# A ring of twenty weight buffers instead of eighteen, and a cap on the loads ahead of a loop

## The chip, the cores and the metric

The kernel runs on one core of a Trainium2 chip. Times are device microseconds (us) of one execution; the metric is the median of several runs.

## The reference

One layer of a streaming encoder, float32, on 256 frames and 16 meta tokens, width 1024. A mixer (differential attention beside a state-space model) and a layer norm come first. Then comes a mixture of 32 experts, of which each token takes four:

```python
gate = xb @ w_gate[e] + b_gate[e]
up = xb @ w_up[e] + b_up[e]
gate = jnp.minimum(gate, SWIGLU_LIMIT)
up = jnp.clip(up, -SWIGLU_LIMIT, SWIGLU_LIMIT)
y = ((up + 1.0) * gate * jax.nn.sigmoid(gate * SWIGLU_ALPHA)) @ w_down[e] + b_down[e]
```

Each expert has three matrices of 1024 x 1024, so 96 matrices of 4 MB are read: 384 MB, once each. A second layer norm ends it.

## The kernel before, in words

**The stream of weights.** Each expert matrix is loaded in four pieces of 1 MB (256 rows of 1024 floats). Experts are sorted by load and worked off as positions t = 0 to 31; a position has three steps w: gate (0), up (1), down (2). `stream` lists the 384 pieces in the order of use: both input steps of position t, then the down step of position t - 1. `place` gives a piece's number in it. `place[28, 2, 3]` is 355 and `place[29, 1, 3]` is 351.

**The ring.** Piece c goes into entry c % NR of `ring` (line 488), where an entry is a half of a buffer slot; NR is 18. The first buffers to be free stand first, since most of them hold the mixer's operands ahead of the stream. `load_to(n)` (line 529) has SP issue pieces until n are out, in order. `chunk` (line 500) issues one (line 522; the last piece in two halves, line 525). Each waits until TensorE has used what lay in the buffer, and SP's queue does everything in program order, so a wait holds all loads behind it.

**Where loads are issued.** In the mixer, `load_to` is called with 2, 4, 6, 10, 12, 16 and 18 (lines 702 to 1001), each time where slots have just come free. In the expert part, every step calls it with the number of its own last piece plus 1 + NR (lines 1298 and 1339): as many pieces are out as the ring holds.

**The order of the engines' work.** The loop at the end of `hybrid_layer` writes it out by hand: for each t, the gate and up steps (`unit_in`), then the tokens of the next group are gathered (`prepare`, line 1118 for the matmuls), then the down step of t - 1 (`out_pos`). A step is `linear`: a matmul that puts in the bias (line 1150), then eight blocks of matmuls on the weights (line 1156), two blocks a piece. `add_rows` (line 1211) and, for the last position, lines 1327 and 1361 add an expert's rows to the tokens.

**The overflow loop.** Experts can get more tokens than their place in the plan has room for. `overflow` (line 1236) reads the count of such leftovers into every engine (line 1237) and runs a hardware loop over them (line 1238). It stands in `out_pos(28)` (LOOP_AT is 28), in the iteration t = 29, behind the loads that the steps of t = 29 call for. With these inputs the count is zero. After it come the two rows of the second layer norm (bc2, by `load`, line 128) and the loads of the last positions.

**Other names.** `Gt` (line 884) holds the gates of the chosen experts; `gates` writes it, `onehots` and `sort_b` read it. `rep` is scratch of `route_c`. The kernel is built with the default scratch space for descriptors of dynamic DMAs (line 1463).

Of the kernel before, what the change touches and what calls it, by code (L numbers as in the profile page):

```python
# [25 lines left out]
NE = 32  # L26
# [21 lines left out]
LOOP_AT = 28  # L48
# [16 lines left out]
def hybrid_layer(ctx, tc, I, out):  # L65
    nc = tc.nc
# [10 lines left out]
    def nb(n=1):  # L77
        b = bank[0]
        if b + n > 8:
            b = 0  # L80
        bank[0] = (b + n) % 8
        return b
# [44 lines left out]
    def load(dst, name, off, dims):  # L127
        return SP.dma_start(dst, pap(I[name], off, dims))
# [192 lines left out]
    for k in range(7):  # L321
        n = min(2 ** k, 68 - 2 ** k)
# [161 lines left out]
    def rows_of(kb):  # L484
        a = 256 * (kb // 2) + kb % 2
        return slice(a, a + 255, 2)

    ring = [(6, 0), (6, 1), (3, 0), (3, 1), (4, 0), (4, 1), (2, 0), (8, 0), (2, 1), (8, 1), (1, 0), (1, 1),
            (5, 0), (0, 0), (5, 1), (0, 1), (7, 0), (7, 1)]
    NR = len(ring)  # L490
    RT, CH, eid, npools = {}, {}, {}, {}
# [6 lines left out]
    place = {x_: c for c, x_ in enumerate(stream)}  # L498

    def chunk(c):  # L500
        t, w, j = stream[c]
        i, half = ring[c % NR]
        if i not in RT:
            if i == 7:
                t_ = npools["b"].tile([128, 4, D], F32, name="wx", tag="slot7")
                RT[i] = [t_[:, 0:2], t_[:, 2:4]]
            elif i in HALVED:
                RT[i] = [slot(f"{i}{c}", [128, 2, D], "wx") for c in "ab"]
            else:
                t_ = slot(i, [128, 4, D], "wx")  # L510
                RT[i] = [t_[:, 0:2], t_[:, 2:4]]
        CH[c] = RT[i][half]
        src = I[("w_gate", "w_up", "w_down")[w]]
        if t < 2:
            srcv = pap(src, t * D * D + j * 256 * D, [[2 * D, 128], [1, 2 * D]])
        else:
            if t not in eid:
                eid[t] = SP.value_load(EI[0:1, t:t + 1], min_val=0, max_val=NE - 1)
            srcv = src[0][ds(eid[t], 1), j * 256:(j + 1) * 256, :].rearrange("o (p k) f -> p (o k f)", p=128)
        dstv = CH[c].rearrange("p k f -> p (k f)")  # L520
        if c < len(stream) - 1:
            SP.dma_start(dstv, srcv)
        else:
            for k in range(2):
                SP.dma_start(dstv[:, k * D:(k + 1) * D], srcv[:, k * D:(k + 1) * D])
# [3 lines left out]
    def load_to(n):  # L529
        while nload[0] < min(n, len(stream)):  # L530
            chunk(nload[0])
            nload[0] += 1


    def split_w(j, s_, l_, ks):
# [75 lines left out]
    def values(h):  # L611
        vT = lw([128, NP], "vT", bufs=2)
        S.activation(vT, proj("v", h, 0), AF.Copy)
        return vT

    def value_rows(h, vT):
        b = nb()
        for blk, n in ((0, 128), (1, 128), (2, 16)):
            T.transpose(PS[:n, b, blk * 128:blk * 128 + 128], vT[:, blk * 128:blk * 128 + n], ident)
        S.activation(vr[:, 0:2, h * 128:(h + 1) * 128], PS[:, b, 0:256].rearrange("p (a e) -> p a e", a=2), AF.Copy)  # L620
        S.activation(vr[:16, 2, h * 128:(h + 1) * 128], PS[:16, b, 256:384], AF.Copy)
# [65 lines left out]
    def lag_b():  # L687
        KS = lt_([128, 4, 128], "KS", tag="y0")
        S.activation(KS, PS[:, kb_].rearrange("p (f c) -> p f c", f=4), AF.Copy)
        V.tensor_add(KS[:, :, 0:32], KS[:, :, 0:32], Dm)  # L690
        for j in range(4):
            for t in range(4):
                dst = ML[32 * t:32 * t + 32, :, j, 32 * t:128]
                srcv = KS[32 * j:32 * j + 32, :, 0:128 - 32 * t]
                if t < 2:
                    V.tensor_copy(dst, srcv)
                else:
                    S.activation(dst, srcv, AF.Copy)

    vt0 = values(2)  # L700
    lag_b()
    load_to(2)
    vt1 = values(3)
    wo0 = slot(3, [128, 4, D], "wo0")
    W_OUT[0] = [wo0[:, k] for k in range(4)]
# [9 lines left out]
    split_w(1, 5, 0, ((2, False, G), (3, False, G)))  # L715
    value_rows(2, vt0)
    value_rows(3, vt1)
    load_to(4)


    cat = mt([128, 8, NT], "cat", FR, tag="hTcat")
# [52 lines left out]
    def out_a(fb):  # L774
        b = nb()
        for j in range(4):
            P = 4 * fb + j
            o = PS[:64, b, j * 128:(j + 1) * 128]
            T.matmul(o, u4[:, P, 4:68], ML[:, fb, j], start=True, stop=False)
            for ri in range(2):  # L780
                T.matmul(o, XS[fb][:, ri, j, 3:67], AB[:, ri, P].rearrange("p t g c -> p (t g c)"),
                         start=False, stop=(ri == 1))
        yt = lt_([64, 512], "yt", bufs=2)
        S.activation(yt.rearrange("p (t a c) -> p a t c", t=4, a=4),
                     PS[:64, b].rearrange("p (a t c) -> p a t c", a=4, t=4), AF.Copy, scale=0.5)
        YT[fb] = yt
# [15 lines left out]
    def out_c(f2):  # L802
        hy, ya = HY[f2]
        for f in range(2):
            V.scalar_tensor_tensor(gy[:, 2 * f2 + f].rearrange("p (c t) -> p t c", t=4), ya[:, f], 1.0, hy[:, f],
                                   op0=OP.add, op1=OP.mult)
# [9 lines left out]
    out_b(0)  # L816
    out_a(2)
    out_a(3)
    load_to(6)
    out_c(0)  # L820
    av_c(1)
    out_b(1)
# [6 lines left out]
    def mix(i, kbs, fs=(0, 1)):  # L829
        for f in fs:  # L830
            for kb in kbs:
                o, q, k, c_ = PS[:, mb + 2 * i + f, :], kb // 4, kb % 4, slice(i * 128, (i + 1) * 128)
                f_ = slice(f * 512, (f + 1) * 512)
                T.matmul(o, cat[:, kb, c_], W_HI[q][k][:, f_], start=(kb == 0), stop=False)
                T.matmul(o, cat[:, kb, c_], W_LO[q][k][:, f_], start=False, stop=False)
                T.matmul(o, cl[q][:, k, c_], W_HI[q][k][:, f_], start=False, stop=(kb == 7))
# [38 lines left out]
    def wt(shape, name, dt=F32, tag=None, bufs=None):  # L875
        return wp.tile(shape, dt, name=name, tag=tag or name, bufs=bufs)
# [4 lines left out]
    jp, io = wt([128, 128], "jp", I32, tag="tabi"), wt([128, 128], "io")  # L881
    tri, one = wt([128, 128], "tri", BF), wt([128, 128], "one", BF)
    P96, s32 = wt([96, NE], "P96", BF), wt([128, 32], "s32")
    lg, M_, Gt, PM, ev, rep = (wt([128, 2, NE], n) for n in ("lg", "M", "Gt", "PM", "ev", "rep"))
    Mb = wt([128, 2, NE], "Mb", BF)
    m8, sm1, nm1 = wt([128, 2, 8], "m8"), wt([128, 2], "sm1"), wt([128, 2], "nm1")
    YC2 = wt([128, 2, D], "yc")
# [4 lines left out]
    for t in range(2):  # L892
        SI[t] = wt([96, 128], "si", BF, bufs=3)
    bc1 = [wt([128, D], "bc1", tag="xg", bufs=2) for _ in range(2)]
    load_to(10)
    load(bc1[0], "ln1_g", 0, [[0, 128], [1, D]])
    load(bc1[1], "ln1_b", 0, [[0, 128], [1, D]])
    load_to(12)


    G.iota(jp, pattern=[[1, 128]], base=0, channel_multiplier=-1)
# [8 lines left out]
    def selector(t, eng):  # L910
        m = max(u[4] for u in UNITS if u[0] == t)
        if t not in SI:
            SI[t] = wt([96, 128], "si", BF, bufs=3)
        eng.tensor_copy(SI[t][:, :m], P96[:, t:t + 1].to_broadcast([96, m]))  # L914
# [22 lines left out]
    def affine1(i, h, eng):  # L937
        hf = hr[:, i, h * 512:(h + 1) * 512]
        eng.tensor_tensor(hf, hf, bc1[0][:, h * 512:(h + 1) * 512], op=OP.mult)
        eng.tensor_tensor(hf, hf, bc1[1][:, h * 512:(h + 1) * 512], op=OP.add)  # L940
# [32 lines left out]
    def places(i):  # L973
        b = nb()
        if i:
            T.matmul(PS[:, b, :NE], one, Mb[:, 0], start=True, stop=False)
        T.matmul(PS[:, b, :NE], tri, Mb[:, i], start=(i == 0), stop=True)
        V.scalar_tensor_tensor(PM[:, i], M_[:, i], -4096.0, PS[:, b, :NE], op0=OP.mult, op1=OP.add)
# [13 lines left out]
    mix(1, (6,), (1,))  # L992
    turn1(0)
    mix(1, (7,), (1,))
    load_to(16)
    mid.close()
    tail = ExitStack()
    npools["b"] = tail.enter_context(tc.tile_pool(name="moeb", bufs=1, side="right", reuse_waits="tile"))
    acc = npools["b"].tile([128, 2, D], F32, name="acc", tag="acc")
    h1T = acc[:, 0].rearrange("p (k c) -> p k c", k=8)  # L1000
    load_to(18)
    affine1(0, 0, G)
    route_a(0)
    norm1(1)
# [7 lines left out]
    places(0)  # L1012
    route_c(1)
    places(1)

    RV, CO, KR = rk[:, 0:NE], rk[:, NE:NE + 3], rk[:, NE + 3:2 * NE + 3]
    tabs = lw([128, 3, 64], "tabs", tag="vT", bufs=2)
# [313 lines left out]
    for t in range(NE):  # L1331
        if 2 <= t + 1 < NE:
            selector(t + 1, G)
        for w in range(2):
            for u in pos_units[t]:
                unit_in(u, w)
            if (t, w) in between:
                between[t, w]()
            load_to(place[t, w, 3] + 1 + NR)
        for g in range(1, NG):  # L1340
            if first_pos[g] == t + 1:
                prepare(g, G)
        if t:
            out_pos(t - 1)
        if t == LOOP_AT + 1:
            bc2 = per.tile([128, 2, D], F32, name="bc2", tag="hr")
            load(bc2[:, 0, :], "ln2_g", 0, [[0, 128], [1, D]])
            load(bc2[:, 1, :], "ln2_b", 0, [[0, 128], [1, D]])

            m = GROUPS[-1][-1][1]  # L1350
            GL = YC2[:, NG % 2].rearrange("p (f c) -> p f c", f=4)
            G.memset(GL, 0.0)  # L1352
            for f in range(128 // m):
                S.activation(GL[f * m:f * m + m, f], GT[NG][:m], AF.Copy)

    (u_,) = pos_units[NE - 1]
    t, g, o, _, m = UNITS[u_]
# [14 lines left out]
    n = r_.shape[2]  # L1372
# [99 lines left out]
```

## Time and profile before

| | |
|---|---|
| median of 3 runs | 1189.6 us (1189.0 to 1190.3) |
| the profiled execution | 1188.67 us |
| its span, first to last instruction | 1186.9 us |
| TensorE matmuls busy | 1038.4 us (87%) |
| VectorE busy | 360.6 us (30%) |
| SP's DMA queue | 88.5% of 16 engines' span |
| read from HBM | 423.50 MB |
| mean granted TensorE clock | 0.952 |

PE is TensorE's matmuls, PEld its weight loads, DVE VectorE, ACT ScalarE, POOL GpSimd, SP the engine that issues all DMAs here (SPq is its queue). In a line of waits, "a <- b: 8.6, 10, 1.6" says that a was idle 8.6 us in all, 10 times, at most 1.6, until b. In a timeline, the bracket gives the idle time before the piece of work and what ended it. [...]

### The profile page before, as it was taken

The page shows a single profiled execution, that of the slowest core. Times are in us where ns is not written, and L with a number is a line of the kernel's source. Part 1 is how long each engine was busy: PE and PEld are TensorE (multiplying, and loading weights), DVE is VectorE, ACT ScalarE, POOL GpSimd, SP SyncE. Part 2 cuts the span into 40 slices and gives each one's busy share as a digit, 9 for nine tenths or more (in the row PEclk, how much of TensorE's full clock was granted, in tenths as well). Part 3 has the DMA queues.
Part 4 walks back from the last instruction along what each step waited for, and adds up shares of the span by engine and source line. Part 5 has one row for each costly group of instructions (what it writes and reads, how often), then busy time and mean ns, then how long its engine had stood idle before and what let it go on. Part 6 is the DMA issues. An engine that isn't in the chain of part 4 may idle for free. (4 is left out here: it accounts for less than half of the span.)

```text
span 1186.9 us, 16400 instructions
## 1 busy us (share of the span) xinstructions
PE 1038.4 (87%) x6572; PEld 529.2 (45%) x6572; DVE 360.6 (30%) x737; ACT 127.2 (11%) x286; POOL 169.6 (14%) x259
## 2 busy tenths in 40 slices
PE   6858798989999988999999987899999999998195
PEld 5646686343543443445434433343443344343042
DVE  7999656222212110221122121121122112121113
ACT  1411442100100000001000000000000000000010
POOL 2990414200200110002001011001101010010001
PEclk9978797989999998999999998999999999999699
DMA  7702478789999999999999999999999897999994
GB/s 214 259 0 76 158 270 332 309 324 423 420 421 421 421 420 421 421 420 420 421 421 421 419 421 421 421 421 421 421 412 404 356 403 274 396 365 422 385 372 196
DMA packets 72314, 425.67 MB, mean 359 GB/s; under 512 B 14925, under 2 KB 15546, under 8 KB 23210
## 3 DMA queue, kind: packets, MB, share of 16 engines
q1 hardware_dynamic: 72234, 424.58, 88.5%
q8 instruction: 53, 0.87, 0.3%
q14 instruction: 27, 0.22, 0.1%
HBM read 423.50 MB, written 1.87 MB: 358 GB/s over the span
## 5 line engine op out<-in xcount | busy, mean ns | idle before, releaser
L1156 PE MATMUL PS<-wx,xgp 128*32 128x256 f32 (+2 forms) x3008 | 464.2, 476 | 14.7 <-DMA wx<-in_w_up 8.6
L1156 PEld LDWEIGHTS PS<-wx,xgp 128*32 128x32 f32 (+2 forms) x3008 | 186.5, 130 | 272.8 <-issue 207.8
L1156 PE MATMUL PS<-wx,yT 128*32 128x256 f32 (+2 forms) x1504 | 231.0, 473 | 21.7 <-DVE yT L1189 17.6
L1156 PEld LDWEIGHTS PS<-wx,yT 128*32 128x32 f32 (+2 forms) x1504 | 92.2, 129 | 148.2 <-issue 95.8
L914 POOL COPY si<-P 96x32 bf16<-96x32 bf16 (+2 forms) x32 | 7.4, 234 | 789.3 <-PE PS L1150 759.8
L1178 DVE TENSOR_SCALAR PS<-PS 128x256 f32<-128x256 f32 (+2 forms) x33 | 22.6, 683 | 191.0 <-PE PS L1156 191.0
L1203 DVE COPY yc<-PS 32x256 f32<-32x256 f32 (+1 forms) x39 | 20.1, 514 | 169.0 <-ACT yc L1205 169.0
L1211 PE MATMUL PS<-yc,gt 128*128 128x512 f32 x120 | 58.6, 620 | 13.6 <-DVE yc L1203 5.7
L1212 DVE TENSOR_TENSOR acc<-PS,acc 128x512 f32<-128x512 f32 x60 | 41.4, 691 | 92.9 <-PE PS L1211 92.7
L1150 PE MATMUL PS<-B,si 96*32 96x256 bf16 (+2 forms) x282 | 39.9, 333 | 32.8 <-SPq L1238 25.9
L1118 PEld LDWEIGHTS PS<-ohp,hr 128*128 128x128 f32 x512 | 63.5, 200 | 8.4 <-issue 8.4
L1118 PE MATMUL PS<-ohp,hr 128*128 128x128 f32 x512 | 65.8, 288 | 0.2 <-DVE ohp L1110 0.2
L1172 DVE TENSOR_SCALAR g<-PS 128x256 f32<-128x256 f32 (+1 forms) x27 | 14.9, 553 | 152.5 <-PE PS L1156 122.1
L1205 ACT ACTIVATE yc<-PS 32x256 f32<-32x256 f32 (+1 forms) x39 | 17.4, 446 | 244.2 <-PE PS L1156 237.8
L1211 PEld LDWEIGHTS PS<-yc,gt 128*128 128x128 f32 x120 | 18.7, 188 | 51.6 <-DVE acc L1212 19.8
L1150 PEld LDWEIGHTS <-si 96*32 96x32 bf16 (+2 forms) x282 | 11.8, 100 | 60.0 <-issue 55.2
L1189 DVE COPY yT<-PS 128x512 f32<-128x512 f32 (+1 forms) x39 | 22.5, 590 | 45.2 <-PE PS L1188 45.2
L1173 ACT ACTIVATE PS<-g 128x256 f32<-128x256 f32 (+1 forms) x27 | 13.2, 491 | 206.3 <-DVE g L1172 206.3
L1108 POOL TENSOR_SCALAR gop<-io,PMs,Gs 128x32 f32<-128x32 f32 (+2 forms) x60 | 33.3, 569 | 0.0
L1172 DVE TENSOR_SCALAR yc<-PS 128x1024 f32<-128x1024 f32 x6 | 7.4, 1225 | 78.3 <-PE PS L1156 78.3
L1122 ACT ACTIVATE xgp<-PS 128x512 f32<-128x512 f32 x16 | 9.6, 597 | 192.5 <-PE PS L1118 192.5
L1110 POOL TENSOR_SCALAR ohp<-io,PMs 128x32 f32<-128x32 f32 (+2 forms) x60 | 24.9, 433 | 0.0
(380 smaller groups left out, 847.9 us busy)
## 6 DMA issues: line engine op xcount, KB each, us to landing
wx<-in_w_gate SPq DMA_DIRECT2D x128, 1024.0 KB, 19.7
wx<-in_w_up SPq DMA_DIRECT2D x128, 1024.0 KB, 19.8
wx<-in_w_down SPq DMA_DIRECT2D x127, 1024.0 KB, 19.7
w_u<-in_w_in SPq DMA_DIRECT2D x2, 1024.0 KB
w_q<-in_w_in SPq DMA_DIRECT2D x1, 2048.0 KB
w_k<-in_w_in SPq DMA_DIRECT2D x2, 1024.0 KB
w_v<-in_w_in SPq DMA_DIRECT2D x1, 2048.0 KB
wo<-in_w_out SPq DMA_DIRECT2D x2, 1024.0 KB
```

The lines of the kernel that those rows point to most:

```text
L1108: eng.tensor_scalar(dst[:, i, o:o + m], iv, pc, gg[:, i, t:t + 1], op0=OP.is_equal, op1=OP.mult)
L1110: eng.tensor_scalar(dst[:, i, o:o + m], iv, pc, None, op0=OP.is_equal)
L1118: T.matmul(PS[:, 4 + h, k * 128:k * 128 + n], hr[:, i, rows_of(db)], oh_[:, i, :n], start=(i == 0), stop=(i == 1))
L1150: T.matmul(o, sel[:, :m], B96[:, w, f * n:f * n + n], start=True, stop=False)
L1156: T.matmul(PS[(f % nf) * m:(f % nf) * m + m, b + f // nf, :n], xT(kb), c[:, f * n:f * n + n], start=False, stop=(kb == 7))
L1172: V.tensor_scalar(g_, r_, 7.0, None, op0=OP.min)
L1178: V.tensor_scalar(r_, r_, 7.0, -7.0, op0=OP.min, op1=OP.max)
L1189: V.tensor_copy(yT[:, 4 * a:4 * a + nk], PS[:, b, :nk * 128].rearrange("p (k s) -> p k s", k=nk))
L1203: V.tensor_copy(d_, s_)
L1205: S.activation(d_, s_, AF.Copy)
L1211: T.matmul(PS[:, b], gt[:n, i * 128:(i + 1) * 128], yc[:n, h * 512:(h + 1) * 512], start=True, stop=True)
L1212: V.tensor_tensor(acc[:, i, h * 512:(h + 1) * 512], PS[:, b], acc[:, i, h * 512:(h + 1) * 512], op=OP.add)
```

## The change

The ring gets a slot 9 in front, two more buffers of 1 MB, so NR is 20. The room (16 KB of each partition) is that of the scratch for dynamic DMAs, which shrinks to 256 bytes; `Gt` moves into the space of `rep`, behind the last use of that. The first two pieces are issued where `load_to` is defined, behind the mixer's own first loads, and every later count in the mixer is two higher. In the iteration ahead of the overflow loop (t = 29), no load goes beyond the eleventh piece after `place[28, 2, 3]`; the call behind the loop makes up for it.

```diff
--- before.py
+++ after.py
@@ -485,7 +485,7 @@
         a = 256 * (kb // 2) + kb % 2
         return slice(a, a + 255, 2)
 
-    ring = [(6, 0), (6, 1), (3, 0), (3, 1), (4, 0), (4, 1), (2, 0), (8, 0), (2, 1), (8, 1), (1, 0), (1, 1),
+    ring = [(9, 0), (9, 1), (6, 0), (6, 1), (3, 0), (3, 1), (4, 0), (4, 1), (2, 0), (8, 0), (2, 1), (8, 1), (1, 0), (1, 1),
             (5, 0), (0, 0), (5, 1), (0, 1), (7, 0), (7, 1)]
     NR = len(ring)
     RT, CH, eid, npools = {}, {}, {}, {}
@@ -530,6 +530,8 @@
         while nload[0] < min(n, len(stream)):
             chunk(nload[0])
             nload[0] += 1
+
+    load_to(2)
 
 
     def split_w(j, s_, l_, ks):
@@ -699,7 +701,7 @@
 
     vt0 = values(2)
     lag_b()
-    load_to(2)
+    load_to(4)
     vt1 = values(3)
     wo0 = slot(3, [128, 4, D], "wo0")
     W_OUT[0] = [wo0[:, k] for k in range(4)]
@@ -715,7 +717,7 @@
     split_w(1, 5, 0, ((2, False, G), (3, False, G)))
     value_rows(2, vt0)
     value_rows(3, vt1)
-    load_to(4)
+    load_to(6)
 
 
     cat = mt([128, 8, NT], "cat", FR, tag="hTcat")
@@ -816,7 +818,7 @@
     out_b(0)
     out_a(2)
     out_a(3)
-    load_to(6)
+    load_to(8)
     out_c(0)
     av_c(1)
     out_b(1)
@@ -881,7 +883,7 @@
     jp, io = wt([128, 128], "jp", I32, tag="tabi"), wt([128, 128], "io")
     tri, one = wt([128, 128], "tri", BF), wt([128, 128], "one", BF)
     P96, s32 = wt([96, NE], "P96", BF), wt([128, 32], "s32")
-    lg, M_, Gt, PM, ev, rep = (wt([128, 2, NE], n) for n in ("lg", "M", "Gt", "PM", "ev", "rep"))
+    lg, M_, PM, ev, rep = (wt([128, 2, NE], n) for n in ("lg", "M", "PM", "ev", "rep"))
     Mb = wt([128, 2, NE], "Mb", BF)
     m8, sm1, nm1 = wt([128, 2, 8], "m8"), wt([128, 2], "sm1"), wt([128, 2], "nm1")
     YC2 = wt([128, 2, D], "yc")
@@ -892,10 +894,10 @@
     for t in range(2):
         SI[t] = wt([96, 128], "si", BF, bufs=3)
     bc1 = [wt([128, D], "bc1", tag="xg", bufs=2) for _ in range(2)]
-    load_to(10)
+    load_to(12)
     load(bc1[0], "ln1_g", 0, [[0, 128], [1, D]])
     load(bc1[1], "ln1_b", 0, [[0, 128], [1, D]])
-    load_to(12)
+    load_to(14)
 
 
     G.iota(jp, pattern=[[1, 128]], base=0, channel_multiplier=-1)
@@ -992,13 +994,13 @@
     mix(1, (6,), (1,))
     turn1(0)
     mix(1, (7,), (1,))
-    load_to(16)
+    load_to(18)
     mid.close()
     tail = ExitStack()
     npools["b"] = tail.enter_context(tc.tile_pool(name="moeb", bufs=1, side="right", reuse_waits="tile"))
     acc = npools["b"].tile([128, 2, D], F32, name="acc", tag="acc")
     h1T = acc[:, 0].rearrange("p (k c) -> p k c", k=8)
-    load_to(18)
+    load_to(20)
     affine1(0, 0, G)
     route_a(0)
     norm1(1)
@@ -1012,6 +1014,7 @@
     places(0)
     route_c(1)
     places(1)
+    Gt = wt([128, 2, NE], "Gt", tag="rep")
 
     RV, CO, KR = rk[:, 0:NE], rk[:, NE:NE + 3], rk[:, NE + 3:2 * NE + 3]
     tabs = lw([128, 3, 64], "tabs", tag="vT", bufs=2)
@@ -1336,7 +1339,8 @@
                 unit_in(u, w)
             if (t, w) in between:
                 between[t, w]()
-            load_to(place[t, w, 3] + 1 + NR)
+            n = place[t, w, 3] + 1 + NR
+            load_to(min(n, place[LOOP_AT, 2, 3] + 1 + 11) if t == LOOP_AT + 1 else n)
         for g in range(1, NG):
             if first_pos[g] == t + 1:
                 prepare(g, G)
@@ -1460,7 +1464,7 @@
     import concourse.bacc as bacc
     from concourse.bass_utils import run_bass_kernel_spmd
 
-    nc = bacc.Bacc("TRN2", target_bir_lowering=False, num_devices=1)
+    nc = bacc.Bacc("TRN2", target_bir_lowering=False, num_devices=1, dynamic_dma_scratch_size=256)
     arrays = {f"in_{n}": a for n, a in layout(inputs).items()}
     I = {n[3:]: nc.dram_tensor(n, a.shape, mybir.dt.from_np(a.dtype), kind="ExternalInput").ap()
          for n, a in arrays.items()}
```

## Rows read from the trace of the kernel before

**Rows 1.** Each engine by stretch: us, busy times, granted clock, DMA share, GB/s

```profile
core 0: us, PE busy (x) PEld busy (x) DVE busy (x) ACT busy (x) POOL busy (x), PEclk, DMA share, GB/s
49.00:101.00 52.00, 29.58 (x147) 24.46 (x146) 49.29 (x76) 7.24 (x23) 41.07 (x28) 0.74 0.13 45
...
422.00:743.40 321.40, 288.95 (x2179) 135.47 (x2167) 62.66 (x105) 20.86 (x43) 28.03 (x67) 0.97 1.01 421
743.40:880.00 136.60, 128.97 (x505) 57.09 (x506) 23.83 (x32) 7.36 (x12) 7.37 (x15) 1.00 1.01 421
876.00:1047.00 171.00, 163.35 (x710) 70.84 (x712) 35.71 (x49) 9.65 (x16) 8.97 (x21) 1.00 0.92 363
1047.00:1124.00 77.00, 51.01 (x474) 23.39 (x466) 12.83 (x24) 4.32 (x10) 5.52 (x14) 0.87 1.01 421
1124.00:1131.00 7.00, 2.79 (x32) 1.31 (x36) 0.00 (x0) 1.66 (x4) 1.11 (x2) 0.50 0.33 96
1131.00:1169.00 38.00, 34.53 (x406) 15.18 (x398) 6.30 (x14) 2.11 (x5) 0.00 (x0) 1.00 1.00 409
```

**Rows 2.** The page's DMA issues: count, size, us from issue to landing

```profile
wx<-in_w_gate SPq DMA_DIRECT2D x128, 1024.0 KB, 19.7
```

**Rows 3.** Waits of SP's queue, 300 to 860 us

```profile
SPq L522 <- DMA wx<-in_w_gate: 134.1, 69, 2.6
...
SPq L522 <- PE PS L1156: 27.0, 32, 5.1
```

**Rows 4.** Waits of PE for pieces, 400 to 743.4 us

```profile
PE PS L1156 <- DMA wx<-in_w_up: 8.6, 10, 1.6
...
PE PS L1156 <- DMA wx<-in_w_gate: 5.3, 6, 1.4
...
PE PS L1156 <- DMA wx<-in_w_down: 3.0, 4, 1.2
```

**Rows 5.** Waits of PE for pieces, 743.5 to 1103 us, the only row

```profile
PE PS L1156 <- DMA wx<-in_w_gate: 0.9, 1, 0.9
```

**Rows 6.** Waits of SP's queue, 876 to 1047 us

```profile
SPq L522 <- PE PS L1156: 136.4, 57, 7.7
```

**Rows 7.** SP's timeline, 40 to 130 us

```profile
47.79 0.48 SPq L128 DMA_DIRECT2D MG<-in_w_glu  x1
101.00 2.20 SPq L128 DMA_DIRECT2D wo<-in_w_out  x2
116.98 1.12 SPq L522 DMA_DIRECT2D wx<-in_w_gate  x2
```

**Rows 8.** SP's timeline around the overflow loop

```profile
1107.33 0.33 SPq L522 DMA_DIRECT2D wx<-in_w_gate  x1
...
1131.04 0.45 SPq L128 DMA_DIRECT2D bc<-in_ln_g  x1
```

**Rows 9.** Waits of SP's queue, 1095 to 1135 us

```profile
SPq L1238 <- SPq L1238: 18.6, 2, 16.1
```

**Rows 10.** PE's timeline around the overflow loop

```profile
1099.83 2.50 PE L1211 MATMUL PS<-yc,gt 128*128 128x512 f32 x5
1128.21 0.40 PE L1150 MATMUL PS<-B,si 96*32 96x256 bf16 x4 [25.87 <-SPq L1238]
```

**Rows 11.** PE's timeline at the end, its last weight pieces

```profile
1160.41 1.07 PE L1156 MATMUL PS<-wx,yT 128*32 128x256 f32 x16 [1.01 <-DMA wx<-in_w_down]
...
1172.24 1.07 PE L1156 MATMUL PS<-wx,yT 128*32 128x256 f32 x16
```

**Rows 12.** Each engine by stretch, as in rows 1

```profile
460.00:465.50 5.50, 5.50 (x8) 2.29 (x7) 0.00 (x0) 0.00 (x0) 0.00 (x0) 0.50 1.02 425
...
718.10:724.80 6.70, 5.70 (x52) 1.96 (x52) 0.85 (x2) 0.39 (x1) 0.00 (x0) 0.50 1.01 422
1160.40:1177.60 17.20, 15.46 (x114) 7.41 (x114) 4.04 (x9) 0.75 (x2) 0.49 (x1) 1.00 0.49 199
```

**Rows 13.** PE's timeline, 714 to 722 us

```profile
718.21 1.94 PE L1156 MATMUL PS<-wx,xgp 128*32 128x256 f32 x16 [1.42 <-DMA wx<-in_w_gate]
```

## The prediction

> **What bounds the kernel now.** I read the stretches first, then the waits of SP's queue and of TensorE, then the timelines around the overflow loop and the end. The weights are 384 pieces of 1 MB (numbered 0 to 383); at the 421 GB/s that the DMA engines hold when they never pause [rows 1], one takes 1.05 MB / 421 = 2.49 us.
>
> In the stretches the reader is to see where that rate is not held: 45 GB/s from 49 to 101 us, 363 GB/s from 876 to 1047, 96 GB/s from 1124 to 1131. From 422 to 880 it is held, and TensorE is nearly always busy too [rows 1]: two bounds take turns. The waits say which. A piece lands 19.7 us after its issue, eight pieces' time [rows 2], and from 300 to 860 SP waits for landings of earlier pieces (134.1 us for those of w_gate alone, against 27.0 for all of TensorE's matmuls) [rows 3], so the transfers set the pace of SP there, not the buffers. TensorE waits for pieces 16.9 us in all between 400 and 743.4 [rows 4], the last time 0.9 us at 743.4, and not again up to the loop [rows 5]. So up to 743 the path is the transfers; from 743 to 1102 it is TensorE. In the part of that where SP is held by buffers (136.4 us of waiting for TensorE's matmuls, 876 to 1047) [rows 6], the transfers idle.
>
> At the loop the roles change again. TensorE is done at 1102.3 and goes on at 1128.2, 25.9 us later [rows 10]. SP issues piece 369 at 1107.33 [rows 8]; 19.7 later it lands, at 1127.0. SP's longest wait in the loop's own code is 16.1 us [rows 9]: the loop runs zero times, but its exit waits until all transfers in flight have landed. So the exit is the landing of the last piece issued ahead of the loop, plus 1.2. While that drains, nothing is issued, and the DMA engines have their hole: 7.0 us at 96 instead of 421 GB/s, 5.4 us lost [rows 1]. After it TensorE catches up until it waits for piece 379 at 1160.41 [rows 11]; the span ends 26.5 us later, at 1186.9. The transfers thus set the end.
>
> **The change part by part.**
>
> *Two pieces early.* Pieces 0 and 1 go out behind w_glu (47.79), ahead of SP's next transfer at 101.00, instead of at 116.98 [rows 7]. Two issues cost SP 1.1 us in a gap of 53 us; they stand behind everything that the preamble is waiting for, and their 5.0 us of transfer fall where the engines move 45 GB/s [rows 1]. Bound: 0, or 5.0 later for the preamble if they shared bandwidth with the 2.6 MB issued just before; I take 0, since those were issued first and SP issues nothing behind them until 101.00. Every later call loads to a count two higher into the buffer that the piece two before had, so the stream is two pieces ahead from there on. Where transfers are the path, that is 2 x 2.49 = 5.0 us, and TensorE takes it over at 743.4, where it last waits for a piece. **-5.0 us**, for TensorE and transfers alike. If TensorE had no wait of 5.0 us to give up it would be less; it has 16.9 [rows 4].
>
> *Two more buffers.* From 876 to 1047 SP may issue a piece two releases earlier. The idle there is 171 x (1 - 363/421) = 23.6 us [rows 1]; two pieces of it are filled. From 1047 on, transfers are unbroken up to the loop (421 GB/s), so this stays as a lead of the stream over TensorE: **-5.0 us** more for the transfers, nothing for TensorE, which has no wait there [rows 5]. Bounds: 0 (if the idle only moves) and -5.0; I take -5.0, because a wait for a buffer is what holds SP in all of this stretch [rows 6].
>
> *The hold.* With 20 buffers SP would put pieces up to 371 ahead of the loop; the hold stops it at 366 (355 is the last that position 28 needs, and eleven more). The exit follows 366 instead of 369: 3 x 2.49 = 7.5 us sooner. With both leads it moves from 1128.2 to 1128.2 - 5.0 - 5.0 - 7.5 = 1110.7. TensorE arrives at 1102.3 - 5.0 = 1097.3, so it still waits 13.4 us, and the drain still ends last. But three more pieces are left for after the exit. Now piece 379, the tenth after it (with the two ln2 loads on the way [rows 8]), comes 1160.4 - 1128.2 = 32.2 us after the exit; then it is the thirteenth, 32.2 + 7.5 = 39.7. Exit plus 39.7 plus 26.5 is 1110.7 + 66.2 = 1176.9, 10.0 less than 1186.9. So the hold itself is worth **0** while transfers set the end: the hole in the transfers only comes sooner. What it takes away is TensorE's lateness: without it, the exit would be at 1123.2, and the 45 us that TensorE now needs from exit to its last piece's end [rows 10, 11] would be the path, 1168.3 against 1110.7 + 39.7 + 12.9 = 1163.3.
>
> *TensorE's clock behind it.* Late in the tail TensorE now waits for pieces 376 to 379 one by one, some 12 us with 1.07 of work in 2.49. The granted clock was 0.50 from 718.1 to 724.8, in a like stretch, and a 1.07 us piece took 1.94 [rows 11, 12, 13]. It may still be low as 379 arrives. Bounds: 0, and 2.5 us as from 460 to 465.5, where a drop of 5.5 us at half clock takes away 5.5 x (1 - 1.07/1.94) [rows 12]. I take **+1.0**: drops came and went in that earlier stretch, which is the nearest. [...]
>
> *The rest.* Gt in the place of rep is written and read after rep's last reader on the same engine, and the smaller scratch is used by no transfer of SP's queue: 0, since VectorE's order hides the first.
>
> **Sum:** -5.0 - 5.0 + 0 + 1.0 = -9.0. The profiled execution took 1188.67, so 1179.7; it stands 0.9 below the median of 1189.6, which becomes **1180.6**. About 0.2% (2.4 us) is what a measurement of this kernel can tell from no change.
>
> **Rivals.**
> 1. *One of the two leads is lost* (the early pieces only fill idle that 101 to 280 had anyway, or the idle of 876 to 1047 only moves). For it: SP's waits are mostly for landings, not buffers [rows 3]. Against it: [rows 6]. -5.0 + 1.0: 1185.6. Chance 0.20.
> 2. *Neither lead counts*, the queue of eight in flight sets all, and the hold is neutral as worked out: 1189.6, no change. Against it: 49 to 101 is empty [rows 1]. Chance 0.08.
> 3. *Slower: the clock stays low to the end.* Place: from piece 376 on. TensorE is busy 15.5 us from 1160.4 to 1177.6 at a clock of 1.00 [rows 12]; at 1.94 for 1.07 that is 12.5 more. It decides if the clock doesn't come back once the waits end; -10.0 + 12.5 = +2.5, 1192.1. [...] Against it: after 25.9 us of idling the clock was back by 1131, 2.8 us after TensorE went on [rows 1, 10]. Chance 0.05.
> 4. *Better: no clock loss and a smaller hole*: 1178.6 to 1179.6, inside the forecast's own range.
> 5. *The exit is not set by the drain* but by an engine that arrives later: the hold then leaves 7.5 us more work behind an exit that has not moved, 1128.2 - 5.0 + 66.2 = 1189.4 of span, +2.5: 1192.1. SP's 16.1 us in the loop [rows 9] speak against it. Chance 0.02.
>
> **How the numbers follow.** The forecast (both leads, clock 0 to 2.5) has 0.65, and gives 1178 to 1183. The range goes up to the first rival with its clock term, 1187, and leaves out rivals 2, 3 and 5: 1178.0 to 1187.0. Faster by over 0.2%: 0.65 + 0.20 = 0.85; within: 0.08; slower: 0.07.
>
> **What would show it.** Right: two pieces issued near 48.5; SP's wait of TensorE in the 876 to 1047 stretch shorter by about 5; TensorE reaching the loop near 1097, its exit near 1111, a wait at the loop of about 13 in place of 25.9; waits for w_down pieces in the tail; the clock's level near the end. Wrong: an exit later than 1115, or a tail from the exit longer than 70 us, or a TensorE that reaches the loop at 1102 as before.

## The result, and the profile after

| | before | changed |
|---|---|---|
| median | 1189.4 us of 6 runs | 1184.0 us of 6 runs |
| all runs | 1189.0 to 1190.3 | 1176.9 to 1186.3 |
| ratio, 95% interval | | 0.9944 [0.9917, 0.9971] |
| profiled execution, span | 1188.7, 1186.9 | 1186.3, 1184.5 |

The changed kernel is 5.4 us faster; 9.0 were forecast. The spread of its runs is new: 9.4 us, against 1.3 for the kernel before and 3.0 to 3.5 where that was timed more often, beside the experiments (one execution of 1279.6 us, at a mean granted clock of 0.829, left aside). The trace of the changed kernel is of the longest of its six executions, that of the kernel before of one that is shorter than all of its six. So the two spans are only 2.4 us apart, and the trace shows what a long execution loses.

The stretches, with the columns of [rows 1]:

```profile
737.40:772.60 35.20, 31.70 (x69) 14.02 (x70) 2.93 (x4) 1.03 (x1) 0.00 (x0) 0.91 1.02 422
876.00:1047.00 171.00, 163.35 (x746) 71.15 (x745) 36.11 (x50) 9.65 (x16) 8.92 (x21) 1.00 0.92 367
...
1110.00:1117.00 7.00, 3.26 (x36) 1.55 (x40) 0.00 (x0) 1.66 (x4) 1.10 (x2) 0.50 0.27 82
...
1142.00:1162.00 20.00, 12.43 (x88) 4.34 (x87) 2.46 (x6) 0.74 (x2) 0.00 (x0) 0.62 0.99 412
```

The first line is position 19 of the experts. The ring stretch, 876 to 1047, still idles (367 GB/s for 363), the hole at the loop has moved from 1124 to 1110 and is as deep as before. New are the clocks: 0.91 around position 19 (the kernel before had 1.00 from 743.4 to 880) and 0.62 in the tail (1.00 before).

SP's timeline where the two early pieces go out, which answers to [rows 7]:

```profile
48.45 1.06 SPq L522 DMA_DIRECT2D wx<-in_w_gate  x2
```

TensorE's timeline at position 19 (line 1159 is line 1156 of before):

```profile
737.42 15.53 PE L1159 MATMUL PS<-wx,xgp 128*128 128x512 f32 x32 [0.87 <-DMA wx<-in_w_gate]
...
756.64 0.38 PE L1153 MATMUL PS<-B,si 96*128 96x512 bf16 x1 [3.47 <-DVE yc L1177]
```

and around the loop, for [rows 10]:

```profile
1094.08 3.91 PE L1214 MATMUL PS<-yc,gt 128*128 128x512 f32 x8 [0.95 <-DVE yc L1206]
1113.74 0.41 PE L1153 MATMUL PS<-B,si 96*32 96x256 bf16 x4 [15.76 <-SPq L1241]
```

and in the tail, for [rows 11]: pieces 376 to 379, and the last, 383.

```profile
1145.62 1.07 PE L1159 MATMUL PS<-wx,yT 128*32 128x256 f32 x16 [2.79 <-DMA wx<-in_w_down]
1148.01 1.94 PE L1159 MATMUL PS<-wx,yT 128*32 128x256 f32 x16 [1.31 <-DMA wx<-in_w_down]
1152.00 1.93 PE L1159 MATMUL PS<-wx,yT 128*32 128x256 f32 x16 [2.06 <-DMA wx<-in_w_down]
1154.50 1.93 PE L1159 MATMUL PS<-wx,yT 128*32 128x256 f32 x16 [0.57 <-DMA wx<-in_w_down]
...
1158.25 3.78 PE L1330 MATMUL PS<-acc,ident 128*128 128x512 f32 x4 [0.84 <-DVE yc L1206]
...
1169.85 1.07 PE L1159 MATMUL PS<-wx,yT 128*32 128x256 f32 x16
```

Position 19's step begins 5.9 us sooner than before (737.42 for 743.31), still on the arrival of a piece, and takes 15.5 us for 14.0; the second step takes 15.6 for 13.9. TensorE reaches the loop at 1098.0 and leaves it at 1113.7, 14.5 sooner. Then all four pieces of the tail are waited for. From the second on they run at half clock, 1.93 for 1.07, and the matmuls behind them too (3.78 for 1.98 in the kernel before). Against the forecast:

| | forecast | changed |
|---|---|---|
| TensorE done ahead of the loop | 1097.3 | 1098.0 |
| exit | 1110.7 | 1113.7 |
| exit to piece 379 | 39.7 | 40.8 |
| piece 379 to the end of the span | 26.5 + 1.0 | 30.0 |

Of the 10.0 us that the transfers were to bring, this execution gives back 3.0 ahead of the exit, 1.1 behind it and 3.5 in the last 30 us: 2.4 is left (1186.9 - 1184.5).

That TensorE reaches the loop so near the forecast is partly luck. Behind position 19 TensorE is only 2.7 us ahead of the kernel before (772.3 for 775.0), where 5.0 were forecast. Another 1.7 come from one step further on, which ran partly at half clock in the trace of the kernel before (first line; granted clock 0.68 from 1072.3 to 1077.6) and not in this one (second line; 1.00 from 1069.6 to 1073.3):

```profile
1072.32 5.35 PE L1156 MATMUL PS<-wx,yT 128*32 128x256 f32 x64 [0.36 <-DVE yT L1189]
```

```profile
1069.66 3.66 PE L1159 MATMUL PS<-wx,yT 128*32 128x256 f32 x64 [0.36 <-DVE yT L1192]
```

### The profile page after: what moved, and what is told of

The parts are those of the page before. It is cut to its first block, busy times and chain, and to the rows that moved or that the text cites. A ratio compares the mean times of both kernels' runs of the same rounds, so it can differ in the third digit from the quotient of the medians.

```text
span 1184.5 us, 16392 instructions
## 1 busy us (share of the span) xinstructions
PE 1042.6 (88%) x6572; PEld 530.0 (45%) x6572; DVE 360.7 (30%) x737; ACT 127.1 (11%) x286; POOL 169.0 (14%) x259
## 3 DMA queue, kind: packets, MB, share of 16 engines
q1 hardware_dynamic: 72234, 424.58, 88.6%
## 5 line engine op out<-in xcount | busy, mean ns | idle before, releaser
L1214 PEld LDWEIGHTS PS<-yc,gt 128*128 128x128 f32 x120 | 18.7, 188 | 51.6 <-DVE acc L1215 19.8
L555 PE MATMUL PS<-u,BAT 128*128 128x68 f32 x64 | 10.6, 331 | 16.3 <-DVE s8b L568 10.8
## 6 DMA issues: line engine op xcount, KB each, us to landing
wx<-in_w_gate SPq DMA_DIRECT2D x128, 1024.0 KB, 19.8
wx<-in_w_up SPq DMA_DIRECT2D x128, 1024.0 KB, 19.8
wx<-in_w_down SPq DMA_DIRECT2D x127, 1024.0 KB, 19.8
```

Source lines behind the costliest of these rows:

```text
L1214: T.matmul(PS[:, b], gt[:n, i * 128:(i + 1) * 128], yc[:n, h * 512:(h + 1) * 512], start=True, stop=True)
```

## The experiments

All were timed beside the kernel before on their own chip; ratios are to that.

| run | median, us | all runs | ratio, 95% interval |
|---|---|---|---|
| e5 changed kernel again | 1183.8 | 1178.9 to 1186.6 | 0.9941 [0.9923, 0.9959] |
| e1 no cap | 1186.4 | 1181.4 to 1188.3 | 0.9965 [0.9954, 0.9976] |
| e2 cap alone | 1191.6 | 1188.1 to 1195.2 | 1.0015 [1.0002, 1.0027] |
| e3 cap of 14 | 1182.0 | 1179.8 to 1182.8 | 0.9928 [0.9915, 0.9941] |
| e4 tail filled | 1181.0 | 1176.6 to 1182.4 | 0.9923 [0.9907, 0.9939] |
| e6 positions 18, 19 filled | 1180.8 | 1178.4 to 1184.1 | 0.9921 [0.9906, 0.9937] |
| e7 no early pieces | 1183.0 | 1180.2 to 1183.9 | 0.9937 [0.9924, 0.9950] |
| e8 cap of 14, 18 and 19 filled, 17 matmuls ahead of the loop | 1178.3 | 1177.6 to 1181.5 | 0.9912 [0.9899, 0.9925] |
| e9 before, 18 and 19 filled | 1188.3 | 1187.4 to 1190.4 | 0.9988 [0.9979, 0.9998] |
| e10 e4 and e6 together | 1178.3 | 1177.7 to 1179.1 | 0.9901 [0.9886, 0.9916] |
| e11 e8 and four more | 1179.5 | 1178.9 to 1180.0 | 0.9912 [0.9899, 0.9926] |

**The cap: e1, e2, e3.** My theory was that the cap is neutral while transfers set the end; the rival, that it is the gain.

e1 takes it off the changed kernel:

```diff
-            n = place[t, w, 3] + 1 + NR
-            load_to(min(n, place[LOOP_AT, 2, 3] + 1 + 11) if t == LOOP_AT + 1 else n)
+            load_to(place[t, w, 3] + 1 + NR)
```

> The changed kernel without the cap on the loads: pieces up to 371 go out ahead of the loop. My theory (transfers set the end with the cap, TensorE without it): the loop's exit comes about 5 pieces of 2.49 us later than with the cap, near 1123 to 1126 us; TensorE then needs its 45 us to its last piece without waiting for pieces 376 to 379, and the span is 1180 to 1182 us (about 1183 us timed), 6 to 7 us under the kernel before, with the clock at 1.00 in the tail. Rival (the cap itself brings the gain): no gain over the kernel before, 1188 to 1190 us. Rival (the cap only costs clock): as fast as the changed kernel's median of 1184.0 us or faster.

e2 puts these two lines into the kernel before, in place of its one.

> The kernel before (18 buffers, nothing early) with the cap of eleven pieces alone. My theory: the exit moves 7.5 us forward (three pieces), near 1120.7 us, and piece 379 comes 7.5 us later after it, so the end stays; with TensorE waiting for pieces 376 to 379 its clock drops in the tail: 1189.5 to 1193 us. Rival (the cap itself brings the gain): 1184 us or less.

e3 changes 11 to 14 in the changed kernel.

> The changed kernel with a cap of fourteen pieces instead of eleven: piece 369 is the last ahead of the loop, as in the kernel before. My theory: the exit is 7.5 us later than with eleven, near 1118 to 1121 us, piece 379 comes at the same time as with eleven, TensorE has hardly any idle time ahead of it, and so keeps its clock at 1.00 behind it: 26.5 us from piece 379 to the end as in the kernel before instead of 30; the time is 1 to 3.5 us below the changed kernel's, 1181 to 1183 us. Rival (the clock in the tail has nothing to do with the waits): the same as the changed kernel, 1184 us, with a clock under 1.00 in the tail.

TensorE's timeline, its first work after the loop, in e1, e2 and e3:

```profile
1129.06 0.40 PE L1153 MATMUL PS<-B,si 96*32 96x256 bf16 x4 [28.79 <-SPq L1241]
```

```profile
1119.91 0.41 PE L1150 MATMUL PS<-B,si 96*32 96x256 bf16 x4 [19.38 <-SPq L1238]
```

```profile
1122.24 0.40 PE L1153 MATMUL PS<-B,si 96*32 96x256 bf16 x4 [23.67 <-SPq L1241]
```

With the cap alone (e2) the exit comes 8.3 us sooner than in the kernel before (7.5 expected), and the time is not shorter but 1.6 us longer. Piece 379 arrives at 1159.8 (1160.4 in the kernel before), and from there to the end it takes 30.2 us for 26.5; as in the changed kernel that piece takes 1.93 us for 1.07 and the matmuls behind it 3.78 for 1.98. So an earlier exit by itself brings nothing, as the sum had it, and costs clock (0.81 from 1142 to 1178, 1.00 in the kernel before).

Without the cap (e1) the exit follows piece 371 and comes at 1129.1, later than the 1123 to 1126 that I expected; in that execution TensorE reached the loop at 1100.3, 2.3 us behind the changed kernel's 1098.0. Still 3.6 us of gain stay in the median. The buffers thus bring most of the gain, and the cap adds some 2.4 on top of them (1184.0 for 1186.4; the two intervals overlap). The rival that the cap is the gain falls; "the cap only costs" has these 2.4 us against it, but isn't excluded.

With a cap of 14 TensorE has no wait for pieces 376 to 379, and the runs lie within 3 us: 1182.0, as expected. Its exit, at 1122.2, is later than the 1118 to 1121 that I expected, and by time alone it can't be told from the changed kernel (the intervals overlap).

In all 13 traces of this document the exit comes 20.3 to 20.9 us after the issue of the last piece ahead of the loop, be that 366, 369 or 371. That is the 19.7 of [rows 2] and 0.6 to 1.2 us more: the exit does follow the landing of that piece, as the prediction had it.

**The clock: e4, e6, e9, e10.** The matmuls added here go to a part of TensorE's output space (PS) that nobody reads then, and nothing uses them; the output is unchanged. They are meant to take the place of idle time.

```diff
+    def idle_mm(n):
+        for _ in range(n):
+            T.matmul(PS[:, 6 + misc[0]], ident, acc[:, 0, 0:512], start=True, stop=True)
+
+    fill = {NE - 2: {0: lambda: idle_mm(2), 2: lambda: idle_mm(1), 4: lambda: idle_mm(1), 6: lambda: idle_mm(1)}}
...
-        r_ = linear(SI[t], 2, in_place(t, 2), transposed(ACT.pop(u), m), m)
+        r_ = linear(SI[t], 2, in_place(t, 2), transposed(ACT.pop(u), m), m, fill.get(t))
```

> The changed kernel with five matmuls of 128x512 that nothing uses, about 1 us each, two ahead of piece 376 and one ahead of each of 377 to 379, in time in which TensorE waits for these pieces; the result stays the reference's. Theory (the low clock behind the waits costs the tail 3.5 us): the clock stays at 1.00 from 376 to the end, 26.5 to 27.5 us from the arrival of piece 379 to the end instead of 30, the time 2 to 3.5 us below the changed kernel's, 1181 to 1182 us. Rival (the tail is longer for another reason, such as a later landing of pieces 380 to 383): 30 us as before, 1184 us.

TensorE's timeline of e4: piece 379, and what follows it.

```profile
1152.82 1.07 PE L1159 MATMUL PS<-wx,yT 128*32 128x256 f32 x16 [0.43 <-DMA wx<-in_w_down]
...
1155.70 1.98 PE L1336 MATMUL PS<-acc,ident 128*128 128x512 f32 x4 [1.16 <-DVE yc L1206]
```

The matmuls behind piece 379 have their times of the kernel before again (1.98 us for the changed kernel's 3.78, each piece 1.07) up to the last on weights, and the span of 1179.3 ends 26.5 us after 1152.8, just as in the kernel before, 3.5 less than in the changed kernel. The exit is where the changed kernel's was (1113.3). So the long tail is the clock, and the rival of a later landing falls.

e6 does the same in positions 18 and 19, with other data (hr for acc) running through:

```diff
+    inside[18, 0] = {k: lambda: idle_mm(1) for k in (2, 4, 6)}
+    inside[18, 1] = {k: lambda: idle_mm(1) for k in (2, 4, 6)}
...
         if w == 0:
+            if t == 19:
+                idle_mm(3)
             ACT[u] = gate_act(r_, m, g)
```

> The changed kernel with nine unused matmuls of about 1 us: six in the steps of position 18, one ahead of each piece that TensorE waits for there, three in the idle 3.5 us between the gate and the up step of position 19. The result stays the reference's. Theory (half clock in position 19 costs TensorE 3.2 us, and that much of the lead is gone at the loop): both steps of position 19 take 14.0 us, TensorE reaches the loop at 1094 to 1095 instead of 1097.7, the exit is 3 us sooner, near 1111, and the time 2.5 to 3.5 us below the changed kernel's, 1181 us. Rival (the lead is lost elsewhere, in the transfers): steps of 14.0 us but the same exit near 1114 and the same time.

Timeline of TensorE in e6, and its stretch of position 19:

```profile
739.16 14.00 PE L1159 MATMUL PS<-wx,xgp 128*128 128x512 f32 x32 [0.87 <-DMA wx<-in_w_gate]
...
1092.58 3.91 PE L1214 MATMUL PS<-yc,gt 128*128 128x512 f32 x8 [0.95 <-DVE yc L1206]
1110.69 0.41 PE L1153 MATMUL PS<-B,si 96*32 96x256 bf16 x4 [14.20 <-SPq L1248]
```

```profile
737.40:772.60 35.20, 33.44 (x98) 15.52 (x91) 4.86 (x6) 1.77 (x3) 0.00 (x0) 1.00 1.01 421
```

The first step takes 14.0 us and the second 13.9, and the exit comes at 1110.7. That this is to the tenth where the sum had put it is chance: the exits of the two traces of the changed kernel, here and in e5, are 0.8 us apart. Since the first step began 1.7 us later than in the changed kernel (739.2 for 737.4), TensorE leaves position 19 and reaches the loop only 1.5 us sooner (1096.5; 1094 to 1095 were expected), yet the exit is 3.0 sooner. Half clock in position 19 thus takes away some of the 3.0 us missing ahead of the exit; that it takes all of them is not shown. How much of the gain of 3 us in time is the changed kernel's own loss, e9 asks, the same nine matmuls in the kernel before:

> The kernel before with the nine unused matmuls in positions 18 and 19 alone. Theory (the kernel before loses little there: in its profile both steps of position 19 ran at full clock, and its transfers have no lead to lose): the kernel before within 1 us, 1188.5 to 1190 us. Rival (the matmuls bring 3 us to whatever kernel, so that the changed kernel's gain of them says nothing on its own loss): 1186 to 1187 us.

It becomes 1.5 us faster (0.2 to 2.5 by its interval): neither "within 1 us" nor 3. The kernel before thus seems to lose some there too. Its own trace has both steps at full clock (14.0 and 13.9 us, granted clock 1.00 from 743.3 to 775.2), but e2's, also with 18 buffers, has the second at 15.6 us. By these medians about half of e6's 3 us is the changed kernel's own; the interval leaves that estimate wide. In e9's own trace the first step still takes 15.7 us, and the granted clock is 0.95 from 742 to 776.

e10 has the matmuls of e4 and of e6:

> The changed kernel, cap of eleven, with the unused matmuls of both earlier runs: nine in positions 18 and 19 and five ahead of pieces 376 to 379. Theory (the two leads of 5.0 us are there in full, and the clock at these two places is all that the changed kernel gives back): exit near 1111, 66 us from there to the end, a span of 1177 us and a time of 1178.5 to 1180 us, 10 us under the kernel before. Rival (another loss besides): 1181 us, as each of the two alone.

Its timeline at the exit and at piece 379:

```profile
1110.53 0.41 PE L1153 MATMUL PS<-B,si 96*32 96x256 bf16 x4 [12.53 <-SPq L1250]
...
1150.84 1.07 PE L1159 MATMUL PS<-wx,yT 128*32 128x256 f32 x16 [0.21 <-DMA wx<-in_w_down]
```

The exit is at 1110.5 (forecast 1110.7), piece 379 comes 40.3 after it (39.7), the span of 1177.3 ends 26.5 later. The sum without its clock term gave 1176.9. The time is 11.5 us under the kernel before, and the four runs lie within 1.4 us, where those of the changed kernel spread over 9. Its interval lies apart from those of the changed kernel, which those of e4 and e6 alone do not. "Another loss besides" falls. Not all half clock is gone in this trace: the first step of position 19 still takes 15.4 us, at a granted clock of 0.72 from 737 to 743.

**The early pieces: e7.** It drops the early `load_to(2)` and sets the mixer's other counts back by two, but for the last, which stays 20.

> The changed kernel without the two early pieces: the mixer's calls load 2, 4, 6, 10, 12 and 16 as in the kernel before, the last one up to 20, so pieces 0 and 1 go out near 117 us and the two new buffers are filled only near 215. Theory (the early issue is what is worth 5.0 us): the stream reaches position 18 with no lead over the kernel before, position 19 begins near 743 instead of 737.4, the time is 5 us above the changed kernel's. Rival (the idle of the transfers from 101 to 280 is enough to catch up, the buffers alone give the lead): position 19 begins at 737 to 739, the time is the changed kernel's within 1 us.

SP's timeline of e7 where the last of the mixer's loads go out, the same pieces (16 to 19) in the kernel before, and TensorE's of e7 at position 19:

```profile
190.39 1.82 SPq L522 DMA_DIRECT2D wx<-in_w_down  x4
```

```profile
192.31 21.15 SPq L522 DMA_DIRECT2D wx<-in_w_down  x4
```

```profile
736.81 15.49 PE L1157 MATMUL PS<-wx,xgp 128*128 128x512 f32 x32 [0.87 <-DMA wx<-in_w_gate]
```

Here my theory fell. All twenty pieces are out at 192 us without the early issue, just as in the changed kernel; position 19 begins at 736.8, sooner than there, and the time is the same. The transfers have idle time enough to bring in two more pieces on the way (246 GB/s from 101 to 215 in this trace, 224 in the kernel before). What makes the lead is that there are two more buffers to fill: in the kernel before pieces 18 and 19 go out only at 211 to 213 us, behind TensorE's first work on the experts' weights (209.4).

**Together: e5, e8, e11.** e5 is the changed kernel unaltered.

> The changed kernel once more, beside the three below on the same chip. Theory (its spread comes from TensorE's clock): a median of 1183 to 1185 us, a spread of 6 us or more, the faster runs with the higher mean clock. In its trace half clock in or behind one of the two gate and up steps of position 19 (15.6 us for 14.0) or behind the waits for pieces 376 to 379. Rival (the spread comes from the transfers): the runs' times do not go with their clock.

Its median and spread are as before, and in the twelve timed runs of this kernel the time goes with the clock, one run excepted: seven with a mean granted clock of 0.948 to 0.951 took 1183.2 to 1186.6 us; of five with 0.953 to 0.960 four took 1176.9 to 1181.3, and one, at 0.955, 1184.7.

e8 joins the cap of 14, the matmuls of e6 and `idle_mm(17)` ahead of `overflow()`; e11 adds one each ahead of three pieces of position 17's down step and one ahead of position 19.

> The cap of fourteen pieces, the nine matmuls of the run with position 18 and 19 filled, and seventeen more of them between the work of position 28 and the loop, so that TensorE comes out of the loop at full clock. Theory (clock on top of the transfers): position 19 in 14.0 us a step, the exit near 1119, the gate step of position 30 in 3.7 us instead of 5.9, no wait for pieces 376 to 379 longer than 2 us and no low clock in the tail: 1178 to 1180 us, with a spread of 3 us or less. Rival (clock is not the cause): 1182 us, as with the cap of fourteen alone.

> The run with everything (cap of fourteen, positions 18 and 19 filled, seventeen matmuls ahead of the loop) with four more unused matmuls: one ahead of each of pieces 2 to 4 of the down step of position 17, one ahead of the gate step of position 19, whose first 3.4 us or more still ran at half clock in that run's profile. Theory: gate step of position 19 in 14.0 us instead of 15.6, 0.5 to 1.5 us below that run's 1178.3 us. Rival (these matmuls come where TensorE does not wait and cost what they take): 1 to 2 us above it.

e8 comes to 1178.3 us; its exit is at 1117.5 and TensorE waits for no piece behind it. Three expectations failed: the first step of position 19 still takes 15.6 us, the first step behind the loop 5.65 instead of 3.7 (TensorE still idles 6.0 us ahead of it), and the spread is 3.8 us. e11 mends the first (13.9 us) and gains nothing: its median is 1.1 us above e8's, its ratio the same. The theory of a gain falls; that the matmuls cost time there, the rival, is not shown, since the difference lies within the runs' spread. e8 and e10 have the lowest medians, 11 us under the kernel before; nothing here tells them apart.

## Why the prediction was right, and where it was wrong

The direction and the range held, and so did the path: transfers up to position 19, TensorE from there to the loop, transfers at the end. The reason given for the first lead did not, and the term for the clock was too small. The time of the changed kernel alone doesn't bear out the forecast: 1184.0 lies nearer to the first rival's 1185.6 than to 1180.6, and its trace shows one of the prediction's own signs of being wrong, a tail of over 70 us from the exit (70.8). What speaks for both leads is e6 and e10. By its steps:

- *Two pieces early, -5.0.* The size held (5.9 us at position 19, and 3.6 to 7.1 in the ten traces with twenty buffers), the reason did not. The step said that the issue into the idle of 49 to 101 puts the stream ahead; e7 has the lead without it. My first rival saw half of this (that the early pieces only fill idle which was there anyway) but concluded that the lead would then be lost.
- *Two more buffers, -5.0.* Held where position 19 is filled: e10's and e6's exits, at 1110.5 and 1110.7, need both leads and the 7.5 us of the cap. In the changed kernel's own trace most of this lead is missing. SP issues piece 366 there 6.5 us sooner than in the kernel before (1093.4 for 1099.9), in e6 9.6; and its waits for TensorE from 876 to 1047 us fell by 2.2 us to 134.2, where the prediction had named about 5 as a sign of being right (6.3 in e6). In that stretch buffers come free at TensorE's pace, and TensorE was late out of position 19.
- *The hold, 0.* Held for the transfers where it stands alone (e2: piece 379 comes 0.6 us sooner). On top of the buffers it brought some 2.4 us in the median; the working had 5.0 (1168.3 for 1163.3), less the clock.
- *The clock, +1.0.* The mis-sized term, and the main reason why 5.4 us came out for 9.0. It measured 3.5 us in the tail of the profiled execution, outside its own bounds of 0 to 2.5: those rested on a drop of 5.5 us, and here the granted clock was 0.50 from 1148 to 1163. A second place was left out of the sum, position 19, where I had taken full clock from the trace of before: the two steps there are 3.2 us longer. In the median run, filling both places brings 5.7 us (1184.0 for e10's 1178.3), of which e9 lets about 1.5 be there without the change.

Not every wait for a piece went with half clock. Of the four pieces waited for in the changed kernel's tail (0.6 to 2.8 us, for 1.07 us of work), three ran at half clock (1.93 to 1.94 us) and the first, behind the longest wait, did not. In the kernel before, the stretch from 1131 to 1169 us, at a granted clock of 1.00, has one such wait, of 1.0 us, and the piece behind it took 1.07. The clock came back in the changed kernel's tail, as I had argued against the third rival, which I gave 0.05: the last piece took 1.07 us again. The twelve runs have a mean granted clock between 0.948 and 0.960, and their times lie up to 9.7 us apart; how much of that is the clock was not measured run by run.

Not tried: a loop that doesn't wait for the transfers in flight (the hole of some 5 us that it makes stays: 82 GB/s for 7.0 us from 1110), and the smaller scratch and the moved Gt without the buffers, which the prediction put at 0. For the scratch the trace shows that SP's queue moved the same 72234 packets and 424.58 MB with it as in the kernel before, and that a piece landed 19.8 us after its issue for 19.7; no run has it alone.

## What to carry to other kernels

More buffers brought 3.6 us here without the cap (e1), in a kernel whose queue waited for a buffer over a long stretch (136.4 us of waits from 876 to 1047); look for such stretches in the waits of the issuing queue, and don't ascribe to an early issue what free room brings anyway. A cap that frees a barrier sooner shifted idle time from ahead of the barrier to behind it, where TensorE then waited piece by piece and ran partly at half clock (e2: 19.4 us ahead for 25.9, 6.1 us of waits for pieces behind it for 1.0, a granted clock of 0.81 from 1142 to 1178 for 1.00): try caps at which neither side waits. Price the clock in every place where a change makes the matmuls wait, and try a few unused matmuls there, counting only waits that are really idle.

## What the runs showed of the hardware that was not expected

Matmuls that nothing uses made the kernel faster: five of them in the tail (e4) or nine in positions 18 and 19 (e6) by 3.0 and 3.2 us in the median, which for each alone is at the edge of what the runs can tell, and both together (e10) by 5.7, which is clear. The spread stayed at 5.9 and 5.7 us with one of the two and was 1.4 in four runs with both, against 7.7 in the six of e5. Four more in places with little idle time (e11) brought nothing.
